# Seven-product pairs for four of the second feed-forward's chunk pairs, two of them from weight sums kept in DRAM, and the issue order of four engines as a table

## The chip, the cores and the metric

The kernel runs on one core of a Trainium2 chip. The metric is device microseconds of one execution. Before the change three runs took 767.77, 767.94 and 768.22 us (median 767.94). PE is TensorE's matmul stream and PEld its weight loads; DVE is VectorE, ACT is ScalarE, POOL is GpSimd, and SP is SyncE, which here only issues DMAs.

## The reference

One residual block on a sequence of 256 tokens with 1024 channels, in float32:

```python
h = rmsnorm(x, ffn1_pre_g);  x = x + 0.5 * rmsnorm(swiglu(h, ffn1_w_in, ffn1_w_down), ffn1_post_g)
h = rmsnorm(x, mix_pre_g)
q_a, f_a, i_a, g_a, q_b, k_b, v_b, f_b, gates = split(h @ w_in)
y_a = (rmsnorm(hgrn2_chunkwise(q_a, f_a, i_a)) * silu(g_a)) @ w_branch_a
y_b = fox_attention(q_b, k_b, v_b, f_b + bias) @ w_branch_b
x = x + rmsnorm((sigmoid(gate_a) * y_a + sigmoid(gate_b) * y_b) @ w_out, mix_post_g)
h = rmsnorm(x, mem_pre_g);   x = x + rmsnorm(mem_cross_attention(h, mem) @ w_mo, mem_post_g)
h = rmsnorm(x, ffn2_pre_g);  x = x + 0.5 * rmsnorm(swiglu(h, ffn2_w_in, ffn2_w_down), ffn2_post_g)

def swiglu(h, w_in, w_down):
    gate, up = split(h @ w_in, 2)
    return (silu(gate) * up) @ w_down          # w_in: 1024 x 5632, w_down: 2816 x 1024
```

`rmsnorm` divides by the root mean square over the channels and multiplies by a gain. The change is about the last line, the second feed-forward.

## The kernel before

**Precision.** Every float32 weight is cut into two parts in the matmul's faster format fp32r: `hi` is the rounded weight and `lo` what is left. The activations are cut in the same way. A product is three matmuls: hi by hi, hi by lo and lo by hi. A matmul here has a 128x128 stationary tile and 512 moving columns (some have 256 or fewer).

**A weight unit.** Weights come in blocks of 128x1024 float32, 512 KB. `load_split` is the path of each: SP issues the load into a `raw` buffer (4 of them), ACT casts it to `hi` (L153), DVE subtracts to get `lo` (L155). There are 8 buffers each for `hi` and `lo`. So SP can issue a load only after DVE has finished with the raw buffer that was filled four loads ago, and a cast can start only when PE has finished with the `hi` of eight units ago. Smaller tiles live in a pool `m4` of 21 buffers; four extra buffers (`sraw`) hold weight sums.

**The feed-forward.** `ffn` is called twice. The 2816 hidden channels are eleven chunks of 256. A chunk's gate and up columns make 512 columns, four weight units. In an ordinary chunk (`act_tok`) each half of the tokens takes 24 matmuls of 512 columns, 48 in all. Then ACT and DVE make silu(gate) times up from the psum tile (`act_evac`: `sg` at L450, `at` at L453 or L455), four PE transposes turn the result (L445, in `flush`), and it is cut into `act`. The product with `w_down` is 12 matmuls per chunk and half (`down`, two more units per chunk), which `between` interleaves with the next chunk's work. The last three chunks' down products (`STAG = 3`) come at the end.

**Pairs.** Two neighbouring chunks can be taken together in `act_pair`: the 2x2 block product (channel halves by chunks) is made with seven block products instead of eight, as in Strassen's and Winograd's scheme. The seven need sums of the activation blocks (`sx`, made once) and of the weight blocks. Each product is 12 matmuls, so a pair takes 84 where two ordinary chunks take 96. The weight sums cost loads and adds instead: a first sum and a second one, and later their sums with other blocks, on DVE (`add`, L596) or, where a pair is in `FETCHED`, partly by accumulating DMAs that POOL issues (L569). Each sum is then cut by L173 and L174 like a raw weight. Three subtractions or additions of psum tiles on DVE (L645, L651, L661) and four copies on ACT (L617, L638 and two others) put the seven products together.

In the second feed-forward (`f2_in`) chunks 0 and 1 are ordinary and taken by halves of the tokens; 2, 5 and 8 are ordinary; (3, 4), (6, 7) and (9, 10) are pairs, all in `FETCHED`.

**The order of the work.** Each engine runs its own list in order. The tile scheduler sets these lists from the order of the code, moved by `tc.high_priority()` and `tc.issue_after(...)`, which the helper `after` and the `behind`, `hold` arguments use; for instance `flush` puts its transposes behind a counted matmul.

**The middle.** Between the feed-forwards lie the mixer's projections (`q_a`, `f_a`, `i_a`, `q_b`, `k_b`, `v_b`, gates; about 200 to 330 us in the profile), its recurrence and attention, the branch products and the memory attention.

Of the kernel before, what the change touches and what calls it, by code (L numbers as in the profile page):

```python
# [35 lines left out]
TOKS = {"f1_in": (3, 8), "f2_in": (2, 5, 8)}  # L36

PAIRS = {"f1_in": (4, 6, 9), "f2_in": (3, 6, 9)}
# [17 lines left out]
FETCHED = {"f1_in": (4, 6, 9), "f2_in": (3, 6, 9)}  # L56
# [11 lines left out]


# [16 lines left out]
def block_kernel(ctx: ExitStack, tc: tile.TileContext, wts, head_in, gf_in, x_in, mem_in, memT_in, cols, rows, fbias, masks, out):  # L86
    nc = tc.nc
    V, S, G, PE = nc.vector, nc.scalar, nc.gpsimd, nc.tensor

    cp = ctx.enter_context(tc.tile_pool(name="consts", bufs=1))  # L90
# [10 lines left out]

    @contextmanager
    def after(i):

        with tc.high_priority(), tc.issue_after(log[min(i, len(log) - 1)]):
            yield
# [37 lines left out]
    def load_split(src, n=512, behind=None, parts=None):  # L144

        raw = wp.tile([P, D], F32, tag="raw", name=nm("raw"), bufs=4)
        hi, lo = parts or parts_of()
        r, h, l = raw, hi, lo
        if n < 512:
            r, h, l = (p.rearrange("p (k n) -> p k n", k=2)[:, :, :n] for p in (raw, hi, lo))  # L150
        loads.append(nc.sync.dma_start(r, src).ins)
        with tc.issue_after(behind[0]) if behind else nullcontext():
            casts.append(S.copy(h, r).ins)  # L153
        with tc.issue_after(behind[1]) if behind else nullcontext():
            los.append(V.tensor_tensor(out=l, in0=r, in1=h.bitcast(F32), op=ALU.subtract).ins)  # L155
        return hi, lo

    def unit(name, i):
        u = _AT[name] + i
        if u not in cache:  # L160
            cache[u] = load_split(wts[u - 4], behind=hold.get(u), parts=place.get(u))
        return cache[u]

# [131 lines left out]
    def table(ins):  # L295

        with tc.issue_after(ins):
            S.activation(warm, ones[:, 0:1], AF.Abs_reciprocal_sqrt)
# [128 lines left out]
    def ffn(w_in, w_dn, X, r2, n_tok, i_row, first_half, second_half=None):  # L427
# [8 lines left out]
        def flush(n):  # L436

            if late:
# [3 lines left out]
                with after(n):  # L442
                    for h in range(2):
                        for j in range(2):
                            PE.transpose(trv[:, j, h * P : (h + 1) * P], ats[c, h][:, j * P : (j + 1) * P], ident)  # L445
                    split(acts[c][:, 0], acts[c][:, 1], trv)
# [87 lines left out]
        def pair_inputs():  # L534
            for k in range(2):
              with tc.issue_after(evs[-1][1]):
                V.tensor_tensor(out=xf[k][:, :, P:], in0=xf[k][:, :, P:], in1=bc(row[:, :P], [P, 4, P], 1), op=ALU.mult)
# [33 lines left out]
        def act_pair(c, between):  # L571
# [40 lines left out]
            sums, both = sums_of_pair.pop(c)  # L612
# [3 lines left out]
            product(b1, of_x(0), splits(sums), True)  # L616
# [3 lines left out]
            add(sums, both)  # L620
# [6 lines left out]
            with tc.issue_after(last_silu[0]) if c - 2 in pairs else nullcontext():  # L627
                u = splits(sums)
# [3 lines left out]
            raw = raws(1, 1)  # L632
            add(sums, raw)
            u = splits(sums)
# [5 lines left out]
            product(b4, of("baed"), splits(raw), False)  # L640
            if c not in FETCHED[w_in]:
                add(both, raw)
            with tc.high_priority():
                t = half_tile("c01")
                V.tensor_tensor(out=t, in0=b4, in1=v, op=ALU.subtract)  # L645
                act_evac(t, c, 0)
            product(b1, of("ad"), splits(both), False)
            S.copy(w, b1)
            with tc.high_priority():
                t = half_tile("c11")  # L650
                V.tensor_tensor(out=t, in0=p5, in1=w, op=ALU.subtract)  # L651
                act_evac(t, c, 1, r2[0], q)
            step_between()
            b0 = trp()
            raw = raws(1, 0)
            m = len(log)
            product(b0, of_x(1), splits(raw), True)
            add(sums, raw)
            with tc.high_priority():
                t = half_tile("c00")  # L660
                V.tensor_tensor(out=t, in0=p1, in1=b0, op=ALU.add)  # L661
                act_evac(t, c + 1, 0)
# [4 lines left out]
            product(b1, of("e"), splits(sums), False)  # L667
            if late[:1] == [c]:
                flush(m + 18)
            with tc.high_priority():  # L670
                silu = act_evac(b1, c + 1, 1, r2[0], q)
# [8 lines left out]
        def pair_loads(c):  # L680
            if c in pairs and c not in sums_of_pair:
                with tc.issue_after(loads[-1]):
                    sums_of_pair[c] = sum_load(c, 0, ((0, 0), (0, 1))), sum_load(c, 1, ((0, 1), (1, 1)))
# [17 lines left out]
        if callable(r2):  # L701
# [4 lines left out]
            for c in range(2):  # L706
                acts[c] = m4([P, 2, 2, T], F32R, "act")
                for h in range(2):
                    with tc.issue_after(casts[-1]):
                        silu = act_evac(outs[c][h], c, h)  # L710
# [3 lines left out]
        for c in range(n_tok, NFF):  # L714
# [42 lines left out]
            if c <= 6 <= last:  # L757
                grow = load_row(i_row)
                if first_half:
                    with tc.issue_after(loads[-1]):  # L760
                        nc.sync.dma_start(masks_s, masks)
# [58 lines left out]
    for kb in range(KB):  # L820
# [3 lines left out]
        for c in range(2):  # L824
            hi, lo = (p[:, kb % 2 * 512 : kb % 2 * 512 + 512] for p in cache[_AT["f1_in"] + 4 * c + kb // 2])
            w = heads[kb][:, HX : HX + 512] if c == 0 else raw1[kb // 2][:, kb % 2 * 512 : kb % 2 * 512 + 512]
            with tc.issue_after(lo_last):
                S.copy(hi, w)
# [5 lines left out]
    def norm_1():  # L834
        with tc.issue_after(loads[X_AT]):
            for h in range(2):
                nc.sync.dma_start(xs[:, h], x_in[:, h])
        with tc.issue_after(loads[-1]):
            nc.sync.dma_start(cols_s, cols)
            nc.sync.dma_start(fb_s, fbias)  # L840
# [7 lines left out]
    def half(X, r, h, g, *ms, into=None, act=True):  # L848

        for i, m in enumerate(ms):  # L850
            with after(m):
                to_T(X, x_blocks(h), h, g, (i,) if len(ms) == 2 else (0, 1), mm if X is X3 and h else trp)
# [30 lines left out]
    with tc.issue_after(iv_last):  # L883
        S.activation(le, le, AF.Exp)
# [13 lines left out]
    for c in range(2):  # L898
        u = chunk("f_a", c)
# [15 lines left out]
    for c in range(2):  # L915
        u = chunk("q_a", c)
# [168 lines left out]
    for c in range(3):  # L1085
        u = [load_split(gf_in[4 * c + i], GF) for i in range(4)]
# [18 lines left out]
    def forget(m):  # L1105
        pf = trp()
        with after(m):
            for h in range(2):
                PE.transpose(pf[0:8, h * P : (h + 1) * P], zf[h], ident)
        V.tensor_scalar(out=fz, in0=pf[0:8, :T], scalar1=fb_s, scalar2=None, op0=ALU.add)  # L1110
        V.scalar_tensor_tensor(out=fa, in0=fz, scalar=-1.0, in1=fz, op0=ALU.mult, op1=ALU.max)
        with tc.issue_after(sig_last):
            logs.append(S.activation(fa, fa, AF.Exp, scale=-1.0).ins)
# [13 lines left out]
    for c in range(2):  # L1127
        for name, lst in (("k_b", kb_), ("q_b", qb_)):
            u = chunk(name, c)
# [21 lines left out]
    with after(r0):  # L1151
        for r in recs:
            r.grow(0)
    for si, ms in enumerate(SETS):
        with after(r0 + R_AT[si]):
            banks = [acc()]
            banks.append(acc() if ms[-1] in (1, 128) else banks[0])
            for j, m in enumerate(ms):
                for r in recs:
                    r.products(m, banks[r.g if m == 128 else j], j == 1)  # L1160
            with tc.issue_after(gf_last[1, 1]) if si == 1 else tc.issue_after(lo_at["k_b", 1]) if ms[-1] == 64 else nullcontext():
                for r in recs:
                    if ms[-1] < 128:
                        r.grow(ms[-1])
            with tc.issue_after(logs[1]) if ms[-1] == 32 else nullcontext():
                for m in ms:
                    for r in recs:
                        r.keep(m, LEVELS.index(m) if m < 64 else None)
        if si == FG:
            with tc.high_priority(), tc.issue_after(recs[1].grown):  # L1170
                forget_sums()
        if si < 2:
            with tc.high_priority(), tc.issue_after(gf_last[R_GROW[si]]):
# [639 lines left out]
```

## Time and profile before

| what | value |
|---|---|
| median of the runs | 767.94 us |
| the profiled execution | 767.82 us |
| its span, in which the engines worked | 765.6 us |
| PE / PEld busy | 756.7 / 642.8 us |
| DVE / ACT / POOL busy | 664.4 / 521.2 / 33.0 us |
| PE matmul records | 4302 |
| second feed-forward, from its transposes to the last pair's end | about 576 to 740 us |

The span is what the profile's views count in; the execution's time is 2.2 us longer. The profile is of one execution and stands 0.12 us below the median. "Idle before, releaser" in a row of a group tells what ended the idle time before its instructions. A PE that is busy all the time in the tenths may still hold small waits, which the timeline of PE and the chain of waits show one by one.

### The profile page before, as it was taken

What the parts mean: (1) busy time and instruction counts of PE and PEld (TensorE: products, weight loads), DVE (VectorE), ACT (ScalarE), POOL (GpSimd) and SP (SyncE); (2) the same over time, 40 slices, a digit from 0 to 9 for tenths busy, and PEclk for the clock granted to TensorE, in tenths of its full rate; (3) what the DMA queues carried; (4) which work ended last, traced back from release to release, by engine and by line L of the source; (5) the groups of instructions that cost most, each with busy time, mean ns of one, the idle gap of its engine ahead of it and who ended that gap; (6) DMA issues with size and microseconds to landing.
All of it is one profiled execution on the core that took longest, in us unless ns stands there. A gap on an engine that the chain in (4) does not pass through costs nothing.

```text
span 765.6 us, 11756 instructions
## 1 busy us (share of the span) xinstructions
PE 756.7 (99%) x4302; PEld 642.8 (84%) x4302; DVE 664.4 (87%) x982; ACT 521.2 (68%) x841; POOL 33.0 (4%) x56
## 2 busy tenths in 40 slices
PE   9999999999999999999999999999999999999996
PEld 8888888888888998898888888888887888888885
DVE  6799998988678898888689899999979899997973
ACT  8667576688774659667666755875968566675762
POOL 0000000000000100200001000001000100000000
PEclk9999999999999999999999999999999999999999
DMA  9778777674745545835668955586386837868641
GB/s 350 235 259 245 214 239 275 182 252 167 233 158 149 185 137 183 284 128 182 189 220 245 267 183 186 175 286 131 114 291 191 257 108 257 236 222 269 176 131 55
DMA packets 47146, 157.88 MB, mean 206 GB/s; under 512 B 5385, under 2 KB 9105, under 8 KB 47089
## 3 DMA queue, kind: packets, MB, share of 16 engines
q1 hardware_dynamic: 43168, 144.83, 55.5%
q0 software_dynamic: 3488, 11.94, 8.7%
q8 instruction: 33, 0.54, 0.3%
q10 hardware_dynamic: 432, 0.37, 0.2%
q14 instruction: 25, 0.20, 0.1%
HBM read 156.06 MB, written 1.06 MB: 205 GB/s over the span
## 4 chain that ended last, share of the span: by engine, by line
PE 85%; DVE 8%; ACT 2%; DMA 2%; issue 1%; DVEq 0%; ACTq 0%
PE mm L100 45%; PE acc L100 33%; PE tr L100 5%; DVE lo L155 2%; DMA raw<-in_wts_dram 2%; PE tr L445 1%; DVE lo L174 1%; ACT hi L153 1%; PE tr L385 1%; DVE xs L421 1%; DVE sraw L1393 1%; DMA head<-in_head_dram 0%; DVE post L416 0%; DVE sx L174 0%; DVE qm L1578 0%
## 5 line engine op out<-in xcount | busy, mean ns | idle before, releaser
L155 DVE TENSOR_TENSOR lo<-raw,hi 128x1024 fp32r<-128x1024 f32 (+1 forms) x188 | 222.3, 1199 | 29.5 <-ACT hi L153 26.2
L153 ACT CAST hi<-raw 128x1024 fp32r<-128x1024 f32 (+1 forms) x188 | 190.9, 1033 | 50.3 <-DMA raw<-in_wts_dram 29.7
L100 PE MATMUL mm<-hi,hlT 128*128 128x512 f32 (+1 forms) x632 | 191.6, 382 | 0.0
L100 PEld LDWEIGHTS mm<-hi,hlT 128*128 128x128 f32 x632 | 116.7, 188 | 20.2
L100 PE MATMUL mm<-lo,hlT 128*128 128x512 f32 (+1 forms) x316 | 119.1, 381 | 0.0
L100 PE MATMUL acc<-hi,act 128*128 128x512 f32 x352 | 113.6, 390 | 0.0
L173 ACT CAST hi<-sraw 128x1024 fp32r<-128x1024 f32 x80 | 83.3, 1052 | 33.9 <-DVE sraw L596 15.6
L174 DVE TENSOR_TENSOR lo<-sraw,hi 128x1024 fp32r<-128x1024 f32 x80 | 96.1, 1221 | 3.8 <-ACT hi L173 3.4
L100 PE MATMUL mm<-hi,sx 128*128 128x512 f32 x280 | 90.8, 391 | 0.0
L100 PEld LDWEIGHTS acc<-hi,act 128*128 128x128 f32 x352 | 66.2, 188 | 13.4
L100 PE MATMUL acc<-lo,act 128*128 128x512 f32 x176 | 69.5, 395 | 0.0
L100 PEld LDWEIGHTS mm<-lo,hlT 128*128 128x128 f32 x316 | 59.3, 188 | 10.0
L100 PEld LDWEIGHTS mm<-hi,sx 128*128 128x128 f32 x280 | 52.5, 188 | 10.9
L100 PE MATMUL acc<-hlT,hi 128*128 128x512 f32 x240 | 60.7, 394 | 0.0
L100 PE MATMUL mm<-lo,sx 128*128 128x512 f32 x140 | 54.9, 392 | 0.0
L100 PEld LDWEIGHTS acc<-hlT,hi 128*128 128x128 f32 x240 | 43.1, 189 | 7.7 <-DVE hlT L373 0.2
L174 DVE TENSOR_TENSOR lo<-raw,hi 128x1024 fp32r<-128x1024 f32 x32 | 38.6, 1221 | 2.1 <-ACT hi L173 2.0
L173 ACT CAST hi<-raw 128x1024 fp32r<-128x1024 f32 x32 | 33.1, 1053 | 8.5 <-issue 3.1
L100 PEld LDWEIGHTS acc<-lo,act 128*128 128x128 f32 x176 | 33.1, 188 | 6.4
L100 PE MATMUL acc<-lo,hT 128*128 128x512 f32 x96 | 37.8, 393 | 0.0
L100 PE MATMUL acc<-hi,hT 128*128 128x512 f32 x96 | 37.7, 392 | 0.1
L100 PE MATMUL acc<-hi,lT 128*128 128x512 f32 x96 | 37.3, 391 | 0.0
(329 smaller groups left out, 1232.4 us busy)
## 6 DMA issues: line engine op xcount, KB each, us to landing
raw<-in_wts_dram SPq DMA_DIRECT2D x215, 512.0 KB, 4.6
sraw<-in_wts_dram SPq DMA_DIRECT2D x32, 512.0 KB, 6.6
sraw<-in_wts_dram POOLq DMA_DIRECT2D x20, 512.0 KB, 5.9
raw<-in_gf_dram SPq DMA_DIRECT2D x12, 344.0 KB, 3.7
head<-in_head_dram SPq DMA_DIRECT2D x7, 392.0 KB, 6.4
grow<-in_rows_dram SPq DMA_DIRECT2D x4, 512.0 KB, 7.6
xs<-in_x_dram SPq DMA_DIRECT2D x2, 512.0 KB, 7.6
cb<-cd POOLq DMA_DIRECT2D x2, 512.0 KB, 4.9
```

What stands on the lines that cost most here:

```text
L100: log.append(PE.matmul(*args, **kw).ins)
L153: casts.append(S.copy(h, r).ins)
L155: los.append(V.tensor_tensor(out=l, in0=r, in1=h.bitcast(F32), op=ALU.subtract).ins)
L173: a = S.copy(hi, src)
L174: b = V.tensor_tensor(out=lo, in0=src, in1=hi.bitcast(F32), op=ALU.subtract)
L385: PE.transpose(blocks[-1][1], src(kb), ident)
L421: summed = V.scalar_tensor_tensor(out=xh, in0=ts[a // 512][:, a % 512 : (b - 1) % 512 + 1], scalar=r, in1=xh, op0=ALU.mult, op1=ALU.add)
L445: PE.transpose(trv[:, j, h * P : (h + 1) * P], ats[c, h][:, j * P : (j + 1) * P], ident)
L1393: V.tensor_tensor(out=x, in0=x, in1=y, op=ALU.add)
```

## The change

**Pairs.** In the second feed-forward chunks 0 to 2 stay ordinary and (3, 4), (5, 6), (7, 8) and (9, 10) are pairs: one pair more, two ordinary chunks fewer. Pairs 3 and 7 get their sums as before (`FETCHED`). Pairs 5 and 9 are in `MADE`.

**Sums kept in DRAM.** For a pair in `MADE` the four weight sums (`sum`, `both`, `sum1`, `sum2`, two units each) are made during the mixer's projections: `make` loads four raw blocks into `ws` tiles of the `m4` pool, makes four adds on DVE, and stores the four results to DRAM tiles `wd`. It is a generator that `load_split` moves on by one step for each weight unit it loads. Pair 5's two calls start in stage `f_a0`, pair 9's two in `k_b1`. In the second feed-forward these pairs then load all seven products' weights (14 units) with `load_split`, from the weights or from `wd`, with no adds and no accumulating DMAs.

**The order.** Every `after`, `issue_after` and `high_priority` is gone. After the program is traced, `issue` reads a table that gives, for PE, DVE, ACT and SP, the whole list as runs of numbers of the traced instructions ("158 149 159+3" is 158, 149, 159, 160, 161), and ties each instruction to the one ahead of it. POOL is not in the table. Of the table one line stands here for each engine.

```diff
-TOKS = {"f1_in": (3, 8), "f2_in": (2, 5, 8)}
-PAIRS = {"f1_in": (4, 6, 9), "f2_in": (3, 6, 9)}
+TOKS = {"f1_in": (3, 8), "f2_in": (2,)}
+PAIRS = {"f1_in": (4, 6, 9), "f2_in": (3, 5, 7, 9)}
-FETCHED = {"f1_in": (4, 6, 9), "f2_in": (3, 6, 9)}
+FETCHED = {"f1_in": (4, 6, 9), "f2_in": (3, 7)}
+MADE = (5,9)
+MADE_AT = {"f_a0": ((5, 0), (5, 1)), "k_b1": ((9, 0), (9, 1))}
+ISSUE = {
+    "PE": (
+        "0+129 154 129+6 155 135+7 156+2 142+7 158 149 159+3 150+4 162+24 190+3 186+3 193+48 189 286+2 241+10 288+2 251+35 290+78 386+2 368+3 388 371+4 389 "
...
+    "DVE": (
+        "1+9 0 11 10 12 242 14 13 15 17 20 16 18+2 21 26 22 27 243 28 23 29 24 30+2 25 32 34 33 35 42 36+5 50 43 41 46+4 44 51 45 67 52 54 53 68 70 55 57 71+2 "
...
+    "Activation": (
+        "0 2+2 5+2 4 7+2 10 9 14 12 11 13 15 1 18 17 22 21 20 24 19 26 23 30 25 29 27 31 33+2 28 35 32 36+3 41 39+2 42 52 16 43+2 53 45 55+2 46+3 57+2 61 49+2 "
...
+    "SP": (
+        "0+5 6 5 8 7 9 15 10 12+2 11 17 14 18+8 27 26 31 28 32 29 33+2 30 35+3 16 38+2 41 40 42 45+3 43+2 54 48+5 55+2 59 57 60 58 63 61+2 64 53 65+21 87 89 86 "
...
+    def issue():
+        traced = [i for i in nc.cur_bb.bb.instructions if i.opcode != "TilePoolBoundary"]
+        for name, runs in ISSUE.items():
+            own = [i for i in traced if i.engine == getattr(mybir.EngineType, name)]
+            order = []
+            for run in runs.split():
+                first, _, n = run.partition("+")
+                order += own[int(first) : int(first) + int(n or 1)]
+            assert len(order) == len(own), (name, len(order), len(own))
+            for before, ins in zip(order, order[1:]):
+                tc.add_manual_dep(ins, before.name, mybir.DependencyInfo(mybir.DependencyClass.NoSync, mybir.DependencyReason.DATA))
-        with tc.issue_after(behind[0]) if behind else nullcontext():
-            casts.append(S.copy(h, r).ins)
-        with tc.issue_after(behind[1]) if behind else nullcontext():
-            los.append(V.tensor_tensor(out=l, in0=r, in1=h.bitcast(F32), op=ALU.subtract).ins)
+        casts.append(S.copy(h, r).ins)
+        los.append(V.tensor_tensor(out=l, in0=r, in1=h.bitcast(F32), op=ALU.subtract).ins)
+        make_step()
         return hi, lo
...
+    def make(c, j):
+        def block(k, n):
+            return wts[_AT["f2_in"] + 4 * (c + 1 - n) + 2 * k + j - 4]
+        t = [m4([P, D], n="ws") for _ in range(4)]
+        def load(i):
+            nc.sync.dma_start(t[i], block(*((0, 0), (0, 1), (1, 1), (1, 0))[i]))
+        def add(i):
+            V.tensor_tensor(out=t[i], in0=t[(0, 1, 0, 2)[i]], in1=t[(1, 2, 2, 3)[i]], op=ALU.add)
+        def store(i):
+            d = dp.tile([P, D], F32, name=nm("wd"))
+            nc.sync.dma_start(d, t[i])
+            made[c, ("sum", "both", "sum1", "sum2")[i], j] = d
+        for i in range(4):
+            yield load(i)
+        for i in range(4):
+            add(i)
+            if i:
+                store(i - 1)
+            yield
+        store(3)
...
+            is_made = w_in == "f2_in" and c in MADE
+            def stored(n):
+                return [load_split(made[c, n, j]) for j in range(2)]
+            def plain(k, n):
+                return [load_split(wts[_AT[w_in] + 4 * (c + 1 - n) + 2 * k + j - 4]) for j in range(2)]
-            product(b1, of_x(0), splits(sums), True)
+            product(b1, of_x(0), plain(0, 0) if is_made else splits(sums), True)
-            add(sums, both)
+            if not is_made:
+                add(sums, both)
-            with tc.issue_after(last_silu[0]) if c - 2 in pairs else nullcontext():
-                u = splits(sums)
+            u = stored("sum") if is_made else splits(sums)
             product(b4, of("de"), u, True)
...
-            product(b1, of("ad"), splits(both), False)
+            product(b1, of("ad"), stored("both") if is_made else splits(both), False)
...
-            product(b1, of("e"), splits(sums), False)
+            product(b1, of("e"), stored("sum2") if is_made else splits(sums), False)
```

**SP at the mixer's stage `f_a`.** This is SP's list of loads, where pair 5's first sums are made (`raw` are the mixer's weight units). Before:

```order
L151 DMA raw_2035<-in_wts_dram 128x1024
L151 DMA raw_2132<-in_wts_dram 128x1024
L151 DMA raw_2138<-in_wts_dram 128x1024
L151 DMA raw_2144<-in_wts_dram 128x1024
L151 DMA raw_2150<-in_wts_dram 128x1024
```

Now:

```order
L254 DMA ws_2023<-in_wts_dram 128x1024
L254 DMA ws_2024<-in_wts_dram 128x1024
L232 DMA raw_2042<-in_wts_dram 128x1024
L254 DMA ws_2025<-in_wts_dram 128x1024
L232 DMA raw_2140<-in_wts_dram 128x1024
L232 DMA raw_2147<-in_wts_dram 128x1024
L232 DMA raw_2156<-in_wts_dram 128x1024
L254 DMA ws_2026<-in_wts_dram 128x1024
L232 DMA raw_2165<-in_wts_dram 128x1024
L261 DMA wd_2154<-ws_2023 128x1024
L232 DMA raw_2265<-in_wts_dram 128x1024
L261 DMA wd_2163<-ws_2024 128x1024
```

Between the mixer's unit loads stand four loads of `ws` blocks, and then the stores of the sums, each of which has to wait for DVE's add.

**SP at the second feed-forward's last pair.** The loads of pair (9, 10), from its first product to its last. Before (four loads into the sum buffers, four raw ones, and down units at L151):

```order
L567 DMA sraw_7354<-in_wts_dram 128x1024
L567 DMA sraw_7356<-in_wts_dram 128x1024
L567 DMA sraw_7358<-in_wts_dram 128x1024
L567 DMA sraw_7360<-in_wts_dram 128x1024
L151 DMA raw_7392<-in_wts_dram 128x1024
L151 DMA raw_7404<-in_wts_dram 128x1024
L567 DMA raw_7457<-in_wts_dram 128x1024
L567 DMA raw_7458<-in_wts_dram 128x1024
L398 DMA grow_7269<-in_rows_dram 128x1024
L567 DMA raw_7538<-in_wts_dram 128x1024
L567 DMA raw_7539<-in_wts_dram 128x1024
```

Now, from the third of its 14 units to the twelfth:

```order
L232 DMA raw_7543<-wd_3139 128x1024
L232 DMA raw_7549<-wd_3936 128x1024
L232 DMA raw_7568<-wd_3157 128x1024
L232 DMA raw_7574<-wd_3954 128x1024
L232 DMA raw_7593<-in_wts_dram 128x1024
L232 DMA raw_7599<-in_wts_dram 128x1024
L232 DMA raw_7623<-wd_3148 128x1024
L232 DMA raw_7629<-wd_3945 128x1024
L232 DMA raw_7655<-in_wts_dram 128x1024
L232 DMA raw_7661<-in_wts_dram 128x1024
```

All of the pair's units now go through the four raw buffers, two for each product, and eight of them come from the stored sums.

**PE behind the last pair.** The last transposes of the hidden activations (L445 before, L562 now) among the down products. Before:

```order
L100 MATMUL acc_6507<-hi_7615,act_6952 128x512
L100 MATMUL acc_6508<-hi_7615,act_6952 128x512
L100 MATMUL acc_6508<-lo_7616,act_6952 128x512
L445 MATMUL tr_7626<-ident,at_7568 128x128 x2
L445 MATMUL tr_7626<-ident,at_7599 128x128 x2
L100 MATMUL acc_6509<-hi_7603,act_6952 128x512
L100 MATMUL acc_6509<-lo_7604,act_6952 128x512
```

Now:

```order
L187 MATMUL acc_6587<-hi_7722,act_7230 128x512
L562 MATMUL tr_7745<-ident,at_7683 128x128
L187 MATMUL acc_6588<-lo_7723,act_7230 128x512
L187 MATMUL acc_6588<-hi_7722,act_7230 128x512
L187 MATMUL acc_6587<-hi_7734,act_7230 128x512
L562 MATMUL tr_7745<-ident,at_7683 128x128
L187 MATMUL acc_6588<-hi_7734,act_7230 128x512
L187 MATMUL acc_6589<-hi_7722,act_7230 128x512
L562 MATMUL tr_7745<-ident,at_7718 128x128 x2
L187 MATMUL acc_6589<-lo_7723,act_7230 128x512
```

The four transposes stood together; two of them now stand apart, with one to four 512-column matmuls between, and the down product's own matmuls have another order.

## The prediction and how it is worked out

> **What bounds the kernel now.** I read the page's busy line and chain first.
>
> ```profile
> span 765.6 us, 11756 instructions
> PE 756.7 (99%) x4302; PEld 642.8 (84%) x4302; DVE 664.4 (87%) x982; ACT 521.2 (68%) x841; POOL 33.0 (4%) x56
> PE 85%; DVE 8%; ACT 2%; DMA 2%; issue 1%; DVEq 0%; ACTq 0%
> ```
>
> PE is busy in 99% of the span and is 85% of the chain that ended last. The profiled execution took 767.82 us, 2.2 more than its span and 0.12 below the median of the runs, so sums against it need no correction. As matmul ends are modelled, I looked next for PE's own waits, by engine and what it waited for (total, times, longest).
>
> ```profile
> PE tr L100 <- PEq L1802: 0.8, 1, 0.8
> PE tr L385 <- DVE xs L421: 0.7, 1, 0.7
> PE tr L445 <- DVE at L455: 0.3, 1, 0.3
> PE acc L1662 <- DVE sm L1652: 0.2, 1, 0.2
> PE acc L100 <- ACT hi L828: 0.2, 1, 0.2
> ```
>
> Apart from the program's start, PE waits 1.4 us in all. So time is won by fewer or cheaper PE instructions, and lost where DVE or the DMAs become too slow to feed PE. How near they are to that, the windows by stage show (us; busy time of PE, PEld, DVE, ACT, POOL; clock; DMA share; GB/s).
>
> ```profile
> 0.00:50.00 50.00, 49.03 (x223) 41.15 (x224) 38.97 (x77) 37.48 (x66) 2.31 (x9) 1.00 0.85 308
> 200.00:285.00 85.00, 85.00 (x932) 77.94 (x931) 71.84 (x121) 55.46 (x83) 3.81 (x15) 1.00 0.52 164
> 285.00:380.00 95.00, 95.00 (x637) 83.29 (x636) 79.26 (x135) 66.15 (x137) 6.76 (x7) 1.00 0.59 196
> 575.00:740.00 165.00, 164.02 (x752) 135.37 (x751) 151.45 (x198) 113.85 (x163) 6.26 (x8) 1.00 0.68 213
> ```
>
> In the second feed-forward (575 to 740) DVE is busy 92% and the DMA engines 68%; in the two middle stretches the shares are 83 to 85% and 52 to 59%.
>
> **PE's work.** One ordinary pair of chunks becomes a seven-product pair: 96 matmuls of 512 columns become 84. Everything else on PE is the same work in another order. The chain gives the price of a matmul where nothing waits (start, us, what).
>
> ```profile
> 632.23 2.72 PE acc L100 x12
> 739.93 19.09 PE acc L100 x84
> ```
>
> 2.72 us for 12 is 0.2267 us, and 84 give 0.2273. The change takes 12 away: **-2.7 us**.
>
> The table also breaks up the groups of transposes. Of 186 with `ident`, none stands alone before; they come in 7 groups of two, 31 of four and 6 of eight. Now 54 stand alone and 44 in twos. Groups of four and eight stand in the chain, one of two in PE's timeline.
>
> ```profile
> 609.51 0.44 PE tr L445 x4
> 589.30 0.87 PE tr L385 x8
> 157.73 0.62 PE L100 MATMUL mm<-hi,sx 128*128 128x512 f32 x2
> 158.19 0.38 PE L445 MATMUL tr<-ident,at 128*128 128x128 f32 x2
> 158.33 0.48 PE L100 MATMUL mm<-lo,sx 128*128 128x512 f32 x1
> 158.64 0.40 PE L100 MATMUL mm<-hi,sx 128*128 128x512 f32 x1
> ```
>
> Four cost 0.44 and eight 0.87, so 0.11 each. In the timeline, the second matmul of the first row starts at 157.96 (one matmul behind 157.73). From there to 158.64 are 0.68 us for two matmuls (0.45) and two transposes, 0.23 or 0.11 each. The line through two, four and eight goes through zero, so a single one should cost 0.11 too: no change. The bounds are 0.057 (a quarter of a 512-column matmul, 54 x 0.055 = 3.0 us gained) and 0.11; I take 0.11, on the nearest row.
>
> [...]
>
> **Small waits on PE.** ACT's list now goes from its first table load straight to the first cast; `xf` and the warm-up, with a table load of its own, come later.
>
> ```profile
> L298 ACT ACT_TABLE_LOAD x4 | 5.1, 1283 | 0.1
> ...
> 4.17 0.51 ACT L832 ACTIVATE xf<-head 128x256 f32<-128x256 f32 x1 [1.50 <-DMA head<-in_head_dram]
> 4.59 0.60 ACT L828 CAST hi<-head 128x512 fp32r<-128x512 f32 x1
> 5.24 0.96 PE L100 MATMUL acc<-hi,hlT 128*128 128x512 f32 x3 [0.18 <-ACT hi L828]
> ```
>
> The cast can start 0.42 us earlier, PE waited 0.18 for it: -0.2. The added table load stands behind the first eight casts; it costs nothing if ACT is ahead of PE there and up to its 1.3 us if not. I take 0, as ACT is busy for 37.5 of the first 50 us while PE is full. The wait for `at` behind the last pair (0.3) keeps its chain, but the matmuls between the last product and its transposes fall from 12 (2.7 us) to 8 (1.8 us); I take -0.2, between a gain of 0.3 and a loss of 0.9. The 0.7 for `xs` is a chain through the norm that no edit shortens: 0. Together **-0.4**.
>
> **DVE and ACT.** In the second feed-forward a fetched pair has 14 casts and splits and 6 adds, a made pair 14 and no adds, two ordinary chunks 8. The groups:
>
> ```profile
> L155 DVE TENSOR_TENSOR lo<-raw,hi 128x1024 fp32r<-128x1024 f32 x176 | 212.1, 1221 | 27.1 <-ACT hi L153 23.9 <-PE acc L100 1.3 <-PE tr L100 1.2
> L596 DVE TENSOR_TENSOR sraw<-sraw,raw 128x1024 f32<-128x1024 f32 x24 | 28.8, 1221 | 1.4 <-DMA raw<-in_wts_dram 1.3
> L645 DVE TENSOR_TENSOR c<-mm,vw 128x512 f32<-128x512 f32 x6 | 4.1, 687 | 0.0
> L153 ACT CAST hi<-raw 128x1024 fp32r<-128x1024 f32 x176 | 182.3, 1051 | 49.5 <-DMA raw<-in_wts_dram 29.7 <-PE mm L100 13.8 <-PE tr L100 3.2
> ```
>
> Chunks 5 to 10: 48 splits and adds before (8 + 2 x 20) and 48 after (20 + 2 x 14). One pair more adds three half tiles of 0.69: DVE +2.1 us, from 151.5 of 165 to 153.6 of 162.3 (95%). ACT gets 6 casts (6.3 us) and 4 copies more, and was idle for 51 us. In the middle DVE gets 16 adds of 1.22, 19.5 us, half of them for pair 5 (200 to 285, 13.2 idle) and half for pair 9 (285 to 380, 15.7 idle): 9.8 us in each. The idle time holds them, so 0; if an add stands ahead of a split that PE is waiting for, it costs up to its 1.22 us.
>
> **DMAs.** The page's queues (packets, MB, share of the span) and those of the second feed-forward, with median us from issue to landing and the spread over `raw` loads there.
>
> ```profile
> q1 hardware_dynamic: 43168, 144.83, 55.5%
> q0 software_dynamic: 3488, 11.94, 8.7%
> ...
> q1 hardware_dynamic: 8744, 31.82, 56.3%
> q0 software_dynamic: 928, 3.21, 11.3%
> raw<-in_wts_dram SPq DMA_DIRECT2D x47, 512.0 KB, 4.5
> sraw<-in_wts_dram SPq DMA_DIRECT2D x12, 512.0 KB, 7.1
> sraw<-in_wts_dram POOLq DMA_DIRECT2D x6, 512.0 KB, 6.5
> DMA to landing us min/median/max: 3.2/4.5/8.8
> ```
>
> SP's queue moved 31.82 MB in 56.3% of 165 us, 1.53 us of the engines per 512 KB; the accumulating queue 3.21 MB in 11.3%, 3.05 us. In the middle come 16 loads and 16 stores: 32 x 1.53 = 49 us in 180, from a share of 0.56 to 0.83. A store of this size is not in the trace; it is bounded by 1.53 and by the 3.05 of the accumulating writes (16 x 1.5 = 24 us more, a share of 0.96); I take 1.53, as it only moves data. In the second feed-forward come 12 loads (28 for two made pairs, less 8 for a fetched pair and 8 for two chunks), less 2 accumulating ones: +12.3 us, from 0.68 to (112 + 12.3) / 162.3 = 0.77.
>
> The narrowest place is the last pair. Its 14 units and the first two down units feed PE one after the other, two per product, 1.36 us each; the last six follow. From its first unit to the last, 22 units pass in 129 matmuls and 14 transposes, 30.8 us, or 1.40 us each. The engines need 1.53, and the four raw buffers set another limit: a buffer is taken for landing, cast and split, 4.5 + 1.05 + 1.22 = 6.8 us, and four give a unit each 1.69. So 22 units need 37.2 us, 6.4 more than PE takes. The cover is what was made ahead. DVE and PE at the same place before:
>
> ```profile
> 722.19 1.22 DVE L174 TENSOR_TENSOR lo<-raw,hi 128x1024 fp32r<-128x1024 f32 x1
> 730.37 0.39 PE L100 MATMUL tr<-lo,hlT 128*128 128x512 f32 x1
> ```
>
> That split ended at 723.41 and PE used it at 730.37, 7.0 us later. Four landed raw units would add 4 x 1.36 = 5.4. 6.4 lies within 7.0 to 12.4: **0**.
>
> **Sum.** 767.82 - 2.7 - 0.4 = **764.7 us**.
>
> **The rivals.** *The raw buffers run dry in the last pair.* If landing takes 6.5 us there, as for POOL's `sraw` loads in the same window, a unit takes (6.5 + 2.27) / 4 = 2.19 us, 22 take 48.2, and 48.2 - 30.8 - 12.4 = 5.0 us are lost: 764.7 + 5.0 = **769.7**, slower. It decides from (30.8 + 7.0) / 22 x 4 - 2.27 = 4.6 us of landing with the small cover, 5.6 with the large one. For it speaks the larger DMA share; against it that the larger landing times are of transfers that queue behind each other, so the bandwidth's 1.53 counts once. Chance 0.18.
>
> *The middle pays back what the end saves.* SP's stores wait for DVE's adds, and weight loads stand behind them on the same queue. Two or three times an add (1.22) plus a late load (1.53) in PE's way is 2.75 to 8; with one such place, 764.7 + 2.75 = **767.5**, no change. For it: DVE at 95% in these stretches after the change. Against it: the share of 0.83 leaves a sixth of the queue free. Chance 0.17.
>
> *Lone transposes are cheaper.* By the bound above 764.7 - 3.0 = **761.7**. For it: none ever stands alone in this trace, so the row is missing. Against it: two cost half of four. Chance 0.13.
>
> **How the numbers follow.** My forecast has 0.52, with a range of its own from 763.7 (all of PE's 1.4 us gone) to 766.0 (the table load's 1.3 not hidden). 0.2% is 1.5 us, about what a measurement can tell here: faster ends at 766.4, slower begins at 769.5. Faster: 0.52 + 0.13 = 0.65; same 0.17; slower 0.18. For 8 in 10 the range goes from 761.6, which holds the cheap transposes, to 769.4, just short of the dry buffers.
>
> **What would show it.** PE's matmul records for 512 columns fall by 12 and `acc` x12 stays at 2.72: then the first term is right. A lone `tr L562` between two 512-column matmuls moves the next one by 0.11 or by 0.06. Of the waits by engine, `PE <- DVE lo` and `PE <- ACT hi` must stay absent from 690 to 725; rows there, with SP waiting for `lo`, are the dry buffers. In the middle DVE should be near 81 of 85 and 89 of 95 us with PE full; PE rows waiting for `lo` near the `ws` adds mean the second rival. It would be wrong altogether if PE's busy time did not fall.

## The result and the profile after

The changed kernel takes 771.85 us (median; 770.70 to 773.92) against 767.36 before in the same comparison: a ratio of 1.0061, 95% interval 1.0049 to 1.0073. That is 4.5 us slower, where 764.7 and faster was forecast. The profiled execution shown here took 773.92 us, the longest of them, so its sums run about 2 us above the median.

The page of the changed kernel, the same three lines as before:

```profile
span 772.0 us, 11838 instructions
PE 758.6 (98%) x4290; PEld 638.7 (83%) x4290; DVE 680.5 (88%) x1001; ACT 526.4 (68%) x852; POOL 30.5 (4%) x54
PE 81%; DMA 8%; DVE 5%; ACT 4%; issue 1%; SPq 0%; DVEq 0%; ACTq 0%
```

PE has 12 matmul records less (4302 to 4290), and yet more busy time. On the chain that ended last, the DMAs went from 2% to 8%. PE's own waits, by engine and what it waited for, beside the 0.8 us of the program's start (total, times, longest):

```profile
PE tr L562 <- DVE at L570: 1.5, 1, 1.5
PE tr L562 <- DVE at L572: 1.0, 1, 1.0
PE tr L503 <- DVE lT L491: 0.8, 1, 0.8
PE acc L187 <- ACT hlT L490: 0.7, 1, 0.7
PE acc L187 <- DVE lo L234: 0.6, 1, 0.6
PE acc L187 <- ACT aux L1196: 0.5, 1, 0.5
PE acc L187 <- ACT f L1193: 0.3, 1, 0.3
PE acc L187 <- DVE G L1316: 0.2, 1, 0.2
```

They are 5.6 us, where they were 1.4. The two largest are in pair 5, the first with stored sums. PE, DVE and ACT there, from their timelines:

```profile
682.87 0.41 PE L562 MATMUL tr<-ident,at 128*128 128x128 f32 x2 [1.54 <-DVE at L570]
684.31 0.48 PE L562 MATMUL tr<-ident,at 128*128 128x128 f32 x1 [1.03 <-DVE at L572]
...
680.56 1.23 DVE L234 TENSOR_TENSOR lo<-raw,hi 128x1024 fp32r<-128x1024 f32 x1 [1.99 <-ACT hi L233]
681.70 0.68 DVE L776 TENSOR_TENSOR c<-pc 128x512 f32<-128x512 f32 x1
682.30 0.41 DVE L570 TENSOR_TENSOR at<-c,sg 128x256 f32<-128x256 f32 x1
...
679.48 1.05 ACT L233 CAST hi<-raw 128x1024 fp32r<-128x1024 f32 x1 [1.78 <-DMA raw<-wd]
680.43 0.58 ACT L774 COPY pc<-mm 128x512 f32<-128x512 f32 x1
```

Read from the bottom: ACT stood 1.78 us before a cast whose unit had not landed, with the copy `pc` behind it; DVE stood 1.99 us for that cast, with `c` and `at` behind its split; PE stood for `at`. The chain of waits leads from there through the raw buffers (start, us, what; pieces under 0.1 us left out):

```profile
657.73 4.67 DMA raw<-in_wts_dram
662.50 2.37 DVE lo L234 x2
664.88 5.95 DMA raw<-wd
670.90 1.06 ACT hi L233
671.99 1.23 DVE lo L234
673.24 6.14 DMA raw<-wd
679.48 1.06 ACT hi L233
```

Load, cast, split, and the next load into the freed buffer: this is the ring of four raw buffers, run dry. A second loss follows at once. The windows of PE's stall and of what comes behind it (busy time of PE, PEld, DVE, ACT, POOL; granted clock; DMA share; GB/s):

```profile
681.00:684.00 3.00, 0.74 (x4) 0.20 (x2) 3.00 (x5) 3.00 (x5) 0.00 (x0) 0.99 0.97 395
684.00:687.00 3.00, 2.69 (x8) 2.10 (x9) 2.57 (x4) 1.38 (x2) 0.84 (x1) 0.50 0.69 283
```

For 3 us the clock was granted at 0.50, worth some 1.5 us more in this execution (an estimate: half of the 3 us). Matmuls at half the clock count as busy (the two from 685.01 to 685.87 take 0.43 us each, for 0.227 elsewhere, with no gap between them), which is most of why PE's busy time rose: in e3 below, whose trace has no such stretch in the feed-forward, it is 756.2 us.

### The profile page after: what moved, and what is told of

Same layout as the page of the kernel before. It is cut to its first block, busy times and chain, and to the rows that moved or that the text cites. A ratio compares the mean times of both kernels' runs of the same rounds, so it can differ in the third digit from the quotient of the medians.

```text
span 772.0 us, 11838 instructions
## 1 busy us (share of the span) xinstructions
PE 758.6 (98%) x4290; PEld 638.7 (83%) x4290; DVE 680.5 (88%) x1001; ACT 526.4 (68%) x852; POOL 30.5 (4%) x54
## 4 chain that ended last, share of the span: by engine, by line
PE 81%; DMA 8%; DVE 5%; ACT 4%; issue 1%; SPq 0%; DVEq 0%; ACTq 0%
PE acc L187 38%; PE mm L187 36%; DMA raw<-in_wts_dram 4%; PE tr L187 3%; DVE lo L234 3%; DMA raw<-wd 2%; ACT hi L233 2%; PE tr L562 1%; DMA ws<-in_wts_dram 1%; DMA head<-in_head_dram 1%; PE tr L503 1%; DVE ws L257 1%; ACT p L1363 1%; PE tr L1374 0%; ACT f L1188 0%
## 5 line engine op out<-in xcount | busy, mean ns | idle before, releaser
L234 DVE TENSOR_TENSOR lo<-raw,hi 128x1024 fp32r<-128x1024 f32 (+1 forms) x208 | 245.6, 1197 | 27.5 <-ACT hi L233 27.1
L233 ACT CAST hi<-raw 128x1024 fp32r<-128x1024 f32 (+1 forms) x208 | 211.0, 1032 | 46.1 <-DMA raw<-in_wts_dram 31.7
L187 PE MATMUL mm<-hi,hlT 128*128 128x512 f32 (+1 forms) x576 | 176.0, 383 | 0.0
L187 PEld LDWEIGHTS mm<-hi,hlT 128*128 128x128 f32 x576 | 105.8, 188 | 18.4 <-ACT hlT L490 0.4
L187 PE MATMUL mm<-lo,hlT 128*128 128x512 f32 (+1 forms) x288 | 109.3, 384 | 0.0
L187 PE MATMUL mm<-hi,sx 128*128 128x512 f32 x320 | 104.0, 393 | 0.0
L292 ACT CAST hi<-sraw 128x1024 fp32r<-128x1024 f32 x70 | 72.7, 1050 | 30.2 <-DVE sraw L712 22.4
L293 DVE TENSOR_TENSOR lo<-sraw,hi 128x1024 fp32r<-128x1024 f32 x70 | 84.0, 1216 | 1.5 <-ACT hi L292 1.1
L187 PEld LDWEIGHTS mm<-lo,sx 128*128 128x128 f32 x160 | 30.2, 189 | 6.3
L187 PEld LDWEIGHTS acc<-hlT,lo 128*128 128x128 f32 x240 | 32.8, 190 | 2.4
```

The costliest lines, as they stand in the source:

```text
L187: log.append(PE.matmul(*args, **kw).ins)
L292: a = S.copy(hi, src)
L293: b = V.tensor_tensor(out=lo, in0=src, in1=hi.bitcast(F32), op=ALU.subtract)
```

## The experiments

Three theories. **Ring**: the four raw buffers can't feed a pair with 14 loaded units, and units come late. **Order**: the supply would do, but the table has put evacuations behind casts and splits that wait. **Making**: the sums made in the middle cost PE time there. All ratios are against the kernel before, measured beside the run.

### e1: the work in the scheduler's order

```diff
  # the kernel before, with after(), issue_after() and high_priority() kept
+ PAIRS, TOKS, FETCHED, MADE, MADE_AT, make(), stored() and plain() of the change
- issue()
```

> The kernel before with the pairs and the stored sums of the change, but with the scheduler's order and all its priorities; the table is left out. If the work costs the time (four raw buffers feeding 14 units a pair, adds and stores in the middle), it is as slow as the change or slower: 770 to 774 us. If the table's order costs it, the 12 matmuls less come through: 764 to 766 us, 2 to 3 below before.

Measured: 788.08 us, ratio 1.0258 (1.0240 to 1.0276). By the ratios (1.0258 and 1.0061) the work in the old manner of ordering is 15 us slower still. So the table is no net loss: it wins back most of what the work costs under the scheduler. The cost is in the work, or in both.

### e2: evacuations ahead of late units

```diff
# ACT's table, pair 5 (traced numbers; 694 = copy pc, 695 = sg, 700 = cast of the late unit)
- 696 697 699 691 700 694 703 704 695
+ 696 697 691 699 694 695 700 703 704
# DVE's table (904 = c, 905 and 909 = at, 908 = c, 915 = split of the late unit)
- 904 911 914 915 908 905 918 909
+ 904 911 905 914 908 909 915 918
# and in pair 9: ACT 752 756 747 750 -> 752 747 756 750; DVE 971 965 968 974 -> 971 965 974 968
```

> The change, with a few rows of the table exchanged on ACT and DVE in pairs 5 and 9: the copy, the sg and the at of an evacuation stand ahead of the cast and split of a unit that lands late. If the order in front of late loads is the cause, PE's waits for at (1.5 and 1.0 us) and the half clock behind them (about 1.8 us) go: 3 to 4.5 us faster than the change, about 767 to 768. If the supply of units is the cause, PE waits for lo or hi of the late units a little later instead: within 1 us of the change, 771 to 772.

Measured: 773.85 us, ratio 1.0083 (1.0062 to 1.0104): nothing gained. The waits by engine:

```profile
PE tr L582 <- DVE at L590: 3.2, 2, 2.7
PE tr L582 <- DVE at L592: 1.6, 2, 1.1
```

The longest wait is now 2.7 us, at 690 us instead of 683, for an `at` that stands behind two splits on DVE (from 687.26, 2.36 us). So the order of these rows alone is not the cause in pair 5: the exchange moved the place at which PE waits.

### e3: four of 14 units into other buffers

The four `sraw` buffers hold no sums of a stored pair; in pair 5 they are free until pair 7's first sums come (from 665 us in the change). Here the units of `sum1` and `both` land in them, with the table unchanged.

```diff
-        raw = wp.tile([P, D], F32, tag="raw", name=nm("raw"), bufs=4)
+        raw = wp.tile([P, D], F32, tag=tag, name=nm("raw"), bufs=4)
...
-                return [load_split(made[c, n, j]) for j in range(2)]
+                return [load_split(made[c, n, j], tag="extra" if n in ("sum1", "both") else "raw") for j in range(2)]
```

> The change, with four of the 14 units of pairs 5 and 9 (sum1 and both) landing in the four extra buffers, which stand empty then, instead of in the raw ring; the order is the same. If the raw ring is what makes units late in pair 5, loads start earlier, the casts wait less for DMA there and PE's waits for at go: 3 to 4.5 us faster than the change, 767 to 768. If the DMA engines are full or only the order counts, within 1 us of the change.

Measured: 766.99 us, ratio 0.9995 (0.9987 to 1.0004). The whole loss of the change is gone, about 5 us with one tag. ACT's waits for loads from 640 to 690 us, in the change:

```profile
ACT hi L233 <- DMA raw<-in_wts_dram: 4.1, 6, 1.5
ACT hi L233 <- DMA raw<-wd: 3.5, 4, 1.8
```

In e3 no row of ACT there waits for a DMA. The windows of the same stretch show what the wider ring did, first the change:

```profile
640.00:650.00 10.00, 10.00 (x46) 8.23 (x46) 9.52 (x12) 6.47 (x10) 0.00 (x0) 1.00 0.48 159
650.00:660.00 10.00, 10.00 (x48) 8.16 (x48) 8.06 (x10) 5.97 (x9) 0.00 (x0) 1.00 0.72 255
660.00:670.00 10.00, 10.00 (x45) 8.24 (x45) 7.55 (x8) 6.96 (x8) 0.00 (x0) 1.00 0.85 296
670.00:680.00 10.00, 10.00 (x45) 8.29 (x45) 6.08 (x6) 5.62 (x7) 0.00 (x0) 1.00 0.97 355
680.00:690.00 10.00, 7.43 (x28) 5.49 (x28) 9.01 (x11) 7.34 (x10) 0.84 (x1) 0.83 0.89 280
```

and e3:

```profile
640.00:650.00 10.00, 10.00 (x48) 8.15 (x47) 9.34 (x13) 8.22 (x12) 0.00 (x0) 1.00 0.46 159
650.00:660.00 10.00, 10.00 (x47) 8.22 (x46) 7.40 (x9) 6.16 (x9) 0.00 (x0) 1.00 0.87 329
660.00:670.00 10.00, 10.00 (x45) 8.26 (x44) 9.35 (x9) 8.15 (x10) 0.00 (x0) 1.00 1.02 404
670.00:680.00 10.00, 10.00 (x47) 8.30 (x46) 7.52 (x9) 7.28 (x9) 0.00 (x0) 1.00 0.82 311
680.00:690.00 10.00, 10.00 (x48) 8.01 (x47) 10.00 (x13) 4.74 (x7) 1.69 (x2) 1.00 0.90 258
```

In both the DMA engines stand half idle until 650. In the change they are then 0.72 to 0.97 busy and too late; in e3 they are 0.87 and 1.02 busy from 650 to 670, so the load is moved ahead, not made less. Landing is hardly faster (median of the raw loads from 655 to 690: 5.6 us in the change, 5.4 in e3): what changed is the number of loads under way, not the time of one. GB/s from 650 to 670 times that landing gives 2.9 transfers of 512 KB under way in the change and 3.8 in e3 (an estimate).

### e7: the other buffers in pair 5 alone

```diff
-  tag="extra" if n in ("sum1", "both") else "raw"
+  tag="extra" if c == 5 and n in ("sum1", "both") else "raw"
```

> As e3, but only pair 5 uses the extra buffers; pair 9 goes through the raw ring alone. If pair 5 was nearly the whole loss (4.5 us of PE's excess there in the change, against 1.0 to 1.5 in pair 9), it stays 0.8 to 1.5 us above e3: 767.8 to 768.5. If the last pair was as costly, as the prediction had it, 769 to 770.

Measured: 768.68 us, ratio 1.0014 (1.0003 to 1.0026). From the change (1.0061) pair 5's ring is worth 0.47% or 3.6 us, and from here to e3 pair 9's is worth 0.19% or 1.5 us. Each ratio's interval is about 0.1% to either side, so the two sizes are rough. The trace agrees with the split: in e7 PE's waits in pair 5 are gone, and 0.9 us of waits for `lo` are left in pair 9.

### e6: the scheduler's order with the other buffers

```diff
  # e1 with the two lines of e3
```

> The run of the work in the scheduler's order (e1, 788 us), with the extra buffers of e3. If the raw ring is what costs it its 20 us, it comes near before, 766 to 770. If the order does, only its waits in pairs 5 and 9 go (3.8 + 4.2 us of PE's 28.8): 779 to 781, and the table is worth the other 12.

Measured: 778.53 us, ratio 1.0148 (1.0130 to 1.0165). The ring is worth 1.1% or 8.4 us in the scheduler's order. It stays 11.4 us above before; e3, the same work with the table, stands at before, so the table takes these away.

### e4 and e8: without the making

Both leave out the 16 loads, adds and stores of the middle, with their numbers in the table; e8 has the buffers of e3 as well.

```diff
-        for i in range(4):
-            yield load(i)
-        for i in range(4):
-            add(i)
-            if i:
-                store(i - 1)
-            yield
-        store(3)
+        for i, n in enumerate(("sum", "both", "sum1", "sum2")):
+            made[c, n, j] = block(*((0, 0), (0, 1), (1, 1), (1, 0))[i])
```

> The change without the making: the 16 loads, 16 adds and 16 stores of the middle are left out, and the second feed-forward loads raw blocks in place of the stored sums (its output is not the reference's). If the making costs PE time in the middle, the waits for f and aux near 331 us (1.1 us and their followers) and for G and lT near 340 and 376 us go: 2 to 3 us faster than the change, 769. If those waits come from the order alone, no change there. Pair 5's waits should stay, as its loads stay.

Measured for e4: 770.18 us, ratio 1.0042 (1.0029 to 1.0055), 1.5 us faster than the change by the ratios and so less than expected. Pair 5's waits for `at` stay (1.7 and 1.0 us in its trace), though its loads come from the weights there and not from the stored sums: reading back stored sums is not what makes units late.

> e3 without the 16 loads, adds and stores of the middle (raw blocks are loaded in place of the stored sums; its output is not the reference's). If the making costs PE 1.7 us of its own, as between the change and e4, it is 1.7 below e3: 765.3. If e4 was faster only because pair 5 was less late in it, it equals e3: 767.0.

Measured for e8: 765.52 us, ratio 0.9977 (0.9966 to 0.9987). The making costs 0.19% with the narrow ring and 0.18% with the wide one, 1.4 to 1.5 us both times, though each with an interval about as wide as itself. That it comes out alike with both rings speaks for a cost of its own.

### e11: the making without its stores

```diff
-            d = dp.tile([P, D], F32, name=nm("wd"))
-            nc.sync.dma_start(d, t[i])
-            made[c, ("sum", "both", "sum1", "sum2")[i], j] = d
+            made[c, ("sum", "both", "sum1", "sum2")[i], j] = block(*((0, 0), (0, 1), (1, 1), (1, 0))[i])
```

> e3 with the loads and adds of the making, but without its 16 stores; raw blocks are loaded in place of the stored sums (its output is not the reference's). The making costs 1.5 us (e3 767.0, e8 765.5). If the stores on SP's queue, which wait for adds with weight loads behind them, cost it, this is at 765.5 to 766. If the adds on DVE or the loads do, it stays at 766.7 to 767.3.

Measured: 765.90 us, ratio 0.9978 (0.9967 to 0.9989), about e8's. So most of the making's cost, 1.3 of 1.4 us by the ratios, with intervals as wide as the difference, seems to be in the 16 stores and not in the adds or loads.

### e5: two repairs of the table at once

```diff
# SP's first loads as before the change (4, 6, 7, 9, 10, 12 = heads, 5, 8, 11 = raw, 15 = cols)
- 4 6 5 8 7 9 15 10 12 13 11
+ 4 5 6 7 8 9 10 11 12 13 15
# ACT near 330 us (332 = copy of f, 333 = copy of aux, 369 and 370 = casts, 341 = cast of qp)
- 369 370 332 341 333
+ 369 332 333 370 341
```

> The run with the extra buffers (e3), with two pieces of the table put right: SP's first 13 loads in the order that they had before the change, and on ACT the copies of f and aux near 330 us ahead of a cast that waits for its load. If these waits are the order's (0.5 us more than before in the head, 0.7 near 330), this is 0.5 to 1.2 us faster than e3: 765.8 to 766.5, and clearly faster than before. If they come from slow landing whatever the order is, no difference to e3, 767.0.

Measured: 771.97 us, ratio 1.0056 (1.0039 to 1.0074): 5 us slower than e3. The first repair was a mistake. PE's wait and, from DVE's timeline, what was late:

```profile
PE acc L207 <- DVE lo L971: 4.3, 1, 4.3
...
20.05 0.17 DVE L1017 TENSOR_TENSOR lmx<-cols_s 128x8 f32<-128x8 f32 x1 [5.72 <-DMA cols_s<-in_cols_dram]
...
20.53 0.69 DVE L971 TENSOR_TENSOR lo<-raw,hi 128x512 fp32r<-128x512 f32 x1
```

The change's DVE list has a small operation on `cols_s` among the first splits, and its SP list loads `cols_s` early for it. With SP's old order, the load comes later and the splits of the head stand behind it.

### e9 and e10: the second repair alone, and a wider ring

e9 is e3 with the exchange on ACT near 330 us; e10 also lands pair 9's `sum2` units in the extra buffers.

> e3 with one exchange in ACT's table: the copies of f and aux near 330 us stand ahead of the cast that waits for its load. The same exchange took PE's excess at 325 to 350 us from 1.6 to 0.65 us in e5, whose loss was all in the head. So 0.7 to 1.0 us faster than e3: 766.0 to 766.3, 1.2 to 1.7 below before. If late loads only move the wait on, it equals e3, 767.0.

Measured for e9: 765.50 us, ratio 0.9973 (0.9961 to 0.9985), faster than before. Against e3 that is 0.22% or 1.7 us, more than expected, with an interval of about 1 us.

```profile
PE tr L207 <- PEq L1919: 0.8, 1, 0.8
PE tr L523 <- DVE lT L511: 0.3, 1, 0.3
```

These are all of its waits on PE: those for `f` and `aux` are gone, and one of 0.3 us is left beside the program's start.

> As e9, with two more units of pair 9 (sum2) in the extra buffers, six of 14 in all. If the raw ring still costs something in the last pair (PE's excess of 0.6 us at 725 to 750 in e3), it is up to 0.5 us faster than e9. If four were enough, no difference.

Measured for e10: 765.17 us, ratio 0.9966 (0.9953 to 0.9979). The fastest kernel here, 2.6 us below before by the ratio. Its interval overlaps that of e9, so what the two further units bring is not shown.

## Why the prediction was wrong

**The 12 matmuls: right.** 12 records less, and a matmul costs what it did. A stretch of the chain after the last pair:

```profile
744.93 6.61 PE acc L187 x29
```

That is 0.228 us each. With the ring and one row repaired, e9 and e10 are 2.1 and 2.6 us below before, with the making's cost still in them: the forecast of 3.1 us below was about the gain that the change could have had. PE's busy time, which had to fall, rose in the change; in e9 it is 755.3 us, 1.4 less than before and not 2.7, and where the rest went is not settled.

**Lone transposes: right to take 0.11, and that rival falls.** PE's timeline of the change:

```profile
86.55 0.39 PE L187 MATMUL acc<-hi,act 128*128 128x512 f32 x1
86.78 0.27 PE L562 MATMUL tr<-ident,at 128*128 128x128 f32 x1
86.81 0.47 PE L187 MATMUL acc<-hi,act 128*128 128x512 f32 x1
87.12 0.39 PE L187 MATMUL acc<-lo,act 128*128 128x512 f32 x1
```

From 86.55 to 87.12 are two matmuls (0.45) and one transpose, so it takes 0.12 us, no less than in a group. If the other lone ones cost 0.01 more than the 0.11 taken, too, the 54 come to about half a microsecond lost (an estimate).

**Small waits: a gain, as forecast; the 0.7 lost belongs to one execution.** The first cast did start earlier (3.92 us, 4.59 before), and PE no longer waited for it. In the profiled execution the second head block landed later (ACT's cast of it starts at 7.48, 6.54 before), and PE waited 0.7 us for `hlT`, which is made from it. The traces of e2, e3, e4 and e7 to e11 have the same rows there; that cast starts at 6.5 to 7.1 us in them, and none has this wait. So it is not a cost of the change. The wait for `xs`, taken to stay, is gone in the change and in e3. Behind the last pair PE no longer waits for `at`, but in the change 0.6 us for `lo`. In e3 PE waits 0.5 us beside the program's start, 0.9 less than before.

**DVE, ACT and the DMAs' amounts: about right.** The adds lie where they were put:

```profile
200.00:285.00 85.00, 85.00 (x811) 77.89 (x811) 78.00 (x121) 52.46 (x82) 4.53 (x16) 1.00 0.72 241
285.00:380.00 95.00, 93.24 (x739) 80.89 (x738) 85.07 (x144) 62.56 (x133) 5.76 (x7) 1.00 0.82 273
...
q1 hardware_dynamic: 49504, 167.90, 62.6%
```

DVE is busy 78 and 85 us, below the 81 and 89 forecast, and the DMA share is 0.72 and 0.82, together 0.77 for the 0.83 forecast. ACT's busy time rose by 5.2 us, for the 6.3 and four copies forecast. The page's queue row gives 1.51 us of the engines per 512 KB with the stores in it. In e3 this row is 63.2% of 764.5 us and in e11, with 16 stores less, 60.4% of 763.7: 21.9 us, or 1.4 for a store. So a store costs about what a load does, as taken.

**The raw ring: the step that failed.** The prediction priced the ring at 1.69 us a unit, found it 6.4 us short in the last pair, and set that to 0, since "6.4 lies within 7.0 to 12.4". Two things were wrong. First the place: "the narrowest place is the last pair" was taken from counting that pair alone. Pair 5's 14 units share SP's queue with down units and with the first four sums of pair 7, and e7 shows 3.6 us there against 1.5 in pair 9. The landing time used, 4.5 us, was the median over the whole second feed-forward, which hid the stretch in which the loads queue; that stretch's row over `raw` in the change (655 to 690 us) reads:

```profile
DMA to landing us min/median/max: 4.0/5.6/7.5
```

By the prediction's own formula that is (5.6 + 2.27) / 4 = 1.97 us a unit in pair 5. Second the cover: in pair 9 the median of the loads from the weights was 4.4 us (705 to 745; 4.1 from the stored sums), about as taken, and about 1.5 us were lost all the same. By the same formula 22 units are then 5.9 us short, so what was made ahead covered about 4.4 us there and not 7.0 or more (an estimate, as rough as the 1.5). The 7.0 was the lead of one split in the kernel before, in another order; why the lead is shorter now is not settled.

The signs that the prediction named would have missed the larger loss: it looked for PE's waits for `lo` and `hi` from 690 to 725, and PE waited at 683, for `at`. SP's wait for `lo`, its other sign, is 30.5 us from 640 to 690 in the change and 28.0 in e3, so it does not tell a ring that is too narrow from one that is wide enough.

The rival that was given 0.18 had the mechanism, the dry raw buffers. That its price of 5.0 is near the 5.1 of both pairs together is luck: it was worked out for the last pair alone and for a landing of 6.5 us there.

**The making: the second rival, at half its price.** 1.4 to 1.5 us were lost, not the 0 of the sum and not 2.75. The rival had SP's stores wait for adds, with weight loads late behind them. From 200 to 385 us SP's and ACT's waits in the change and, last, ACT's in e11 fit that:

```profile
SPq L261 <- DVE ws L257: 6.1, 6, 2.2
ACT hi L233 <- DMA raw<-in_wts_dram: 7.8, 9, 2.1
...
ACT hi L252 <- DMA raw<-in_wts_dram: 2.2, 2, 1.7
```

The evidence is thin: without any stores ACT's wait ranges from the 2.2 of e11 to 4.3 before the change and 4.7 in e8. The time to landing of a `raw` load hardly changed (median from 285 to 380 us: 4.6, 4.3 before, 4.7 in e11). Whether PE pays for the order of the queue or for the fuller DMA engines (a share of 0.82 from 285 to 380 us in the change, 0.68 in e11) is not shown. Which of PE's waits the stores lengthen is not settled either. The wait for `aux` near 330 us is gone in e11's trace and in e9's, but e8's trace, without any making, still has it (0.5 us).

**The order of ACT's rows: no term.** The sum had nothing for the order of the table beyond the transposes and the first cast. Near 330 us ACT stands 1.01 us before a cast whose load is late, with the copies of `f` and `aux` behind it, and e9's exchange of these rows won 1.7 us against e3. In the kernel before PE did not wait there.

**The chances.** The two rivals on the slow side were treated as excluding each other. They are two places with causes of their own, and both came: -2.7 + 5.1 + 1.5 gives 3.9 above before, where 4.5 were measured. With intervals of about 1 us on the measured terms that is no proof that nothing else is in it: the small waits gained and the order near 330 us are left out, and the making's cost and that of the order may overlap. The chance that at least one of two separate losses comes true should have stood against the one sure gain.

## What to carry to other kernels

Work moved from adds on the chip to loads needs buffers for the loads (four more took away 3.6 us in pair 5 and 1.5 in pair 9): compare the time in which a unit is used with landing, cast and split over the number of buffers, for each stretch in which loads bunch, with the landing time of that stretch. Where a list is fixed by hand, a late transfer stops everything behind it on each engine (for one unit of pair 5 ACT stood 1.78 us, DVE 1.99 and PE 1.54); first widen the supply: in pair 5, with late units, an exchange of rows only moved the wait (e2), while near 330 us, where other work stood behind one late load, it paid (e9). And when a list is edited, every operation that waits for a moved load has to be followed too (the `cols_s` load in e5).

## What was not expected of the hardware

A short stall cost twice here. In the change PE was idle for 1.54 and 1.03 us within 3 us, and the clock was then granted at 0.50 for the next 3 us (684 to 687). In e2 one wait of 2.7 us was followed by this window:

```profile
690.00:695.00 5.00, 4.99 (x17) 3.80 (x18) 5.00 (x6) 1.63 (x2) 0.85 (x1) 0.66 0.99 306
```

In e1 one wait of 2.2 us was followed by a granted clock of 0.66 over 5 us (345 to 350) as well; over its whole profiled execution it was 0.993, where the runs of the kernel before beside it have 0.997 to 0.999. It did not always follow: in e4 PE waited 1.74 and 1.03 us at the same place, and the clock stayed at 1.00 (0.998 over that execution, 0.996 over the change's). Single waits of 0.7 us were not followed by it either: behind the one for `hlT` at 8 us it was 1.00 from 9 to 12 us, and behind the one for `xs` before the change 1.00 from 577 to 582. What decides whether it follows is not shown: 2.6 us in two pieces was followed by it in the change, 2.8 us in two pieces was not in e4.
